# Multiplying by w_out with seven products of quarter sums, its weight sums made ahead

## The chip, the cores and the metric

The kernel runs on one core of a Trainium2 chip. The metric is the device time of one execution in microseconds (us). Three timed runs of the kernel before gave 1209.68, 1209.86 and 1210.95 us, so its median is 1209.86 us. A separate profiled execution gives the spans, waits and durations below. Engines are named as in the profile: PE (matrix products and transposes), PEld (its weight loads), DVE (vector arithmetic), ACT (copies and functions), POOL (a second, slower elementwise engine), SP (the queue that issues nearly every DMA). SBUF is the on-chip memory, PSUM the eight banks that PE writes into; a bank holds 128 x 512 numbers.

## What is computed

```python
h = concat(meta_tokens, x)                       # 16 + 1024 tokens, width 1024
# mixer, on u = rmsnorm(h)
z = u @ w_in                                     # split: a, q, k, v, r, lr, ga, gb
y_a = (pool(a) @ w_pool_mix * pool_scale) @ w_pool_out
o   = rmsnorm(gla_chunked(q, k, v, log_a)) * silu(r)
y_b = o @ w_gla_out
m   = sigmoid(ga) * y_a + sigmoid(gb) * y_b      # 1024 x 1024
h   = h + m @ w_out                              # the product that is changed
# MLP
h   = h + square(relu(rmsnorm(h) @ w_ff1)) @ w_ff2
out = rmsnorm(h)[16:]
```

All of it is float32. A product is taken as three passes: each operand is split into a high part (rounded) and a low part (the rest), and high x high, high x low and low x high are added in one bank (`mm3`, lines 281 to 287). So every 128 x 128 x 512 block costs three matmuls, and every operand costs one ACT copy for the high part and one subtraction for the low part.

## The kernel before

The program is written as a list of steps. PE runs in the order in which the steps are written; for the other engines the framework's scheduler chooses an order, with earlier code first. An instruction passed through `keep_in_program_order` is placed behind the instruction that was written before it on the same engine.

**Stage one** (steps `one`, until about 385 us). Norm, transposes, the value projection, then four `a_block`s, two `decays`, four `mix_block`s and two `k_block`s (line 720), and then `pairs_of_projections` (line 853), which already takes its part of `w_in` by seven products of sums (Strassen's scheme in Winograd's form). `differences` (line 692) makes the sums of the input that these products need; the tile pair `t2h`, `t2l` (for the product called P4) is one of them. Weights come through a ring of depth two (`Ring`, lines 57 to 94) by way of two buffers `raw`.

**Attention** (`gla`, line 1277). While PE waits inside the recurrence, it is given filler: four `ya_block`s and four `yb_block`s for the first half of the tokens (h=0). A `yb_block(j, h)` (line 1172) makes two 128-wide columns of m for 512 tokens: twelve matmuls each, then on DVE `gl = (1+gl)*b` (L1195) and `gl += ml` (L1196), then the split: ACT high part (L1199), DVE low part (L1200). `gl` and `ml` are pairs of 256 KB tiles that `ask` (line 1127) loads into a set of small buffers; it always leaves two of these free.

**The merge and w_out** (steps `rest`, from `merge_open`, line 1313, to about 588 us). Eight small buffers hold the pairs (`t1`, `o`). PE takes the four `yb_block`s of the second half of the tokens (h=1, order 2, 3, 0, 1) and sixteen `out_tile(t, ch)` (line 1362): 128 tokens by 512 columns, eight blocks deep, 24 matmuls each, 384 in all. `load_wo` splits w_out in eight pieces of 128 x 1024: ACT L1344, DVE L1345. Bank group `mm` has three banks, `ms` three. `out_tile` adds the bank to x in `acc` (L1379); after the second column half `layer_norm` and `turn_tile` (line 1386, eight transposes) prepare the quarter sums for w_ff1.

**MLP** (`ff1`, `ff2`). Both products go by seven products of sums. PE runs them without a gap but for the first fifteen microseconds.

Of the kernel before, what the change touches and what calls it, by code (L numbers as in the profile page):

```python
# [14 lines left out]
P = 128  # L15
# [81 lines left out]
class Raw:  # L97
# [11 lines left out]
    def load(self, ap, n):  # L109
# [13 lines left out]
def kernel(  # L123
# [55 lines left out]
    h_dram = dp.tile([8, P, D], F32, name="h_dram")  # L179
    hf_dram = [dp.tile([NPAIR, P, HALF], F32, name=f"hf{m}_dram") for m in range(7)]  # L180
# [425 lines left out]
    def decays(p):  # L606
        def fn():
# [6 lines left out]
            if p:  # L614
                act.activation(gnorm, gnorm, ACT.Copy, scale=0.5)
# [6 lines left out]
    def pool_open():  # L622
# [4 lines left out]
        lr_turn()  # L627
        act.activation(S["gu"], wgu, ACT.Copy)
# [91 lines left out]
    for f, i in ((a_, 0), (d_, 0), (a_, 1), (d_, 1), (m_, 0), (a_, 2), (m_, 1), (a_, 3), (m_, 2), (k_, 0), (m_, 3)):  # L720
        f(i)
# [365 lines left out]
    def gla_open():  # L1087
        left.pop_to(S["left_t"])
        right.pop_to(0)
        S["yg"] = {h: right.push(f"yg{h}", [P, 2, HEADS, HALF], F32R) for h in (1, 0)}  # L1090
# [9 lines left out]
        wanted[:] = [("a", d, h) for d in range(8) for h in range(2)] + [("b", d, 0) for d in range(8)]  # L1100
# [67 lines left out]

    KEPT = (2, 3)
    kept = {}  # L1170

    def yb_block(j, h):
        def fn(wb=None):
# [7 lines left out]
            yg = S["yg"][h]  # L1181
            for e in range(2):
                d, w = 2 * j + e, slice(e * P, (e + 1) * P)
                ask()
                gl, ml = take("b", d, h)
# [11 lines left out]
                th = MH[h][:, d]  # L1197
                tl = ML[h][:, d]
                act.activation(th, gl, ACT.Copy, scale=0.5)  # L1199
                dve.scalar_tensor_tensor(tl, gl, 0.5, f32(th), ALU.mult, ALU.subtract)  # L1200
# [132 lines left out]

    def load_wo(ch, kk):
        def fn():
            wo = S["wo"][ch][:, :, 2 * kk : 2 * kk + 2]
            c = slice(ch * HALF, (ch + 1) * HALF)
            src = w_out[kk * 256 : (kk + 1) * 256, c].rearrange("(k p) c -> p k c", p=P)
            if ch:
                r = raw.load(src, D).rearrange("p (k c) -> p k c", k=2)  # L1340
            else:
                r = S["acc"][:, 4 + kk].rearrange("p (k c) -> p k c", k=2)
                nc.sync.dma_start(r, src)
            act.activation(wo[:, 0], r, ACT.Copy)  # L1344
            dve.tensor_tensor(wo[:, 1], r, f32(wo[:, 0]), ALU.subtract)  # L1345
# [3 lines left out]
    step(rest, merge_open)
    def wo1_open():  # L1350
        raw.back()
        left.pop_to(S["left2"])
        right.pop_to(0)
        S["u2p"] = right.push("u2p", [P, 2, HALF], F32)
        raw.lend(right.push("rawx0", [P, D], F32))
        S["right_ff"] = right.mark()
        S["wo"].append(right.push("wo1", [P, 2, KT, HALF], F32R))


    ORDER = (0, 4, 1, 5, 2, 3, 6, 7)  # L1360

    def out_tile(t, ch):
        def fn():
            half, at = t // 4, (t % 4) * P
            wo = S["wo"][ch]
            if ch == 0 and t < 6:
                x_again(t + 2)
# [371 lines left out]
```

## Time and profile before

| | |
|---|---|
| median of the timed runs | 1209.86 us (1209.68 to 1210.95) |
| the profiled execution | span 1209.1 us from its first to its last instruction, 18303 instructions; no other time is given for it |
| busy | PE 1194.4, PEld 993.1, DVE 837.5, ACT 574.4, POOL 79.1 us |
| mean granted clock of PE | 0.998 |
| w_out matmuls (L285, L286, L287 with `wo`) | 128 each, from 490.1 to 587.9 us |
| yb matmuls, both halves (with `yg`) | 64 each for three lines, from 447.3 us |

A line of a group reads: line in the code, engine, operation, output <- inputs, shape, count | busy us, mean ns of one | idle time before it and who ended it. A line of the timeline reads: start us, duration us, engine, line, and so on, and in brackets the idle time before it with its releaser. Matmul ends are modelled, so what counts for PE is the distance from one start to the next.

### The profile page before, as it was taken

The page shows a single profiled execution, that of the slowest core. Times are in us where ns is not written, and L with a number is a line of the kernel's source. Part 1 is how long each engine was busy: PE and PEld are TensorE (multiplying, and loading weights), DVE is VectorE, ACT ScalarE, POOL GpSimd, SP SyncE. Part 2 cuts the span into 40 slices and gives each one's busy share as a digit, 9 for nine tenths or more (in the row PEclk, how much of TensorE's full clock was granted, in tenths as well). Part 3 has the DMA queues.
Part 4 walks back from the last instruction along what each step waited for, and adds up shares of the span by engine and source line. Part 5 has one row for each costly group of instructions (what it writes and reads, how often), then busy time and mean ns, then how long its engine had stood idle before and what let it go on. Part 6 is the DMA issues. An engine that isn't in the chain of part 4 may idle for free.

```text
span 1209.1 us, 18303 instructions
## 1 busy us (share of the span) xinstructions
PE 1194.4 (99%) x6775; PEld 993.1 (82%) x6775; DVE 837.5 (69%) x1369; ACT 574.4 (48%) x1014; POOL 79.1 (7%) x97
## 2 busy tenths in 40 slices
PE   9999999999999999999999999999999999999997
PEld 7999877878778887788788888888888888888886
DVE  6636567565686669726887767677675887887686
ACT  7546444444456124305655545455464444444554
POOL 0000062323320000000000000000000000000000
PEclk9999999999999999999999999999999999999999
DMA  8223253534348978812255444444479963333532
GB/s 245 77 60 123 91 133 110 166 110 146 112 138 296 315 218 268 284 32 87 88 161 168 151 139 157 148 160 151 152 253 318 348 229 98 98 100 91 173 96 88
DMA packets 151385, 192.79 MB, mean 159 GB/s; under 512 B 12216, under 2 KB 86256, under 8 KB 151296
## 3 DMA queue, kind: packets, MB, share of 16 engines
q1 hardware_dynamic: 151136, 191.56, 49.5%
q8 instruction: 53, 0.87, 0.3%
q14 instruction: 36, 0.29, 0.1%
q10 hardware_dynamic: 160, 0.07, 0.0%
HBM read 128.66 MB, written 62.93 MB: 158 GB/s over the span
## 4 chain that ended last, share of the span: by engine, by line
PE 68%; DVE 3%; issue 1%; DMA 1%; ACT 1%; DVEq 0%; ACTq 0%
PE b_oa L287 5%; PE b_oa L285 5%; PE b_oa L286 5%; PE b_y L285 4%; PE b_y L286 4%; PE b_y L287 4%; PE b_mm L285 4%; PE b_mm L287 4%; PE b_mm L286 4%; PE b_ob L287 4%; PE b_ob L285 4%; PE b_ob L286 4%; PE b_z L286 3%; PE b_z L285 3%; PE b_z L287 3%; PE b_sc L285 2%
## 5 line engine op out<-in xcount | busy, mean ns | idle before, releaser
L774 ACT ACTIVATE w1h<-raw 128x512 fp32r<-128x512 f32 x106 | 65.8, 622 | 51.2 <-PE b_sc L286 21.2
L285 PE MATMUL b_sc<-th,w1h 128*128 128x512 f32 x216 | 85.4, 395 | 0.4 <-ACT u2p L1522 0.4
L285 PE MATMUL b_z<-th,w1h 128*128 128x512 f32 x216 | 84.9, 393 | 0.4 <-DVE c L893 0.4
L775 DVE TENSOR_TENSOR w1l<-raw,w1h 128x512 fp32r<-128x512 f32 x106 | 72.5, 685 | 18.0 <-ACT w1h L774 18.0
L286 PE MATMUL b_sc<-tl,w1h 128*128 128x512 f32 x216 | 84.8, 393 | 0.0
L286 PE MATMUL b_z<-tl,w1h 128*128 128x512 f32 x216 | 84.2, 390 | 0.4 <-DVE tl L1408 0.4
L287 PE MATMUL b_sc<-th,w1l 128*128 128x512 f32 x216 | 84.4, 391 | 0.0
L287 PE MATMUL b_z<-th,w1l 128*128 128x512 f32 x216 | 84.1, 389 | 0.0
L774 ACT ACTIVATE w1h<-fs 128x512 fp32r<-128x512 f32 x81 | 51.1, 630 | 67.0 <-PE b_y L286 33.6
L775 DVE TENSOR_TENSOR w1l<-fs,w1h 128x512 fp32r<-128x512 f32 x81 | 57.7, 712 | 23.7 <-ACT w1h L774 23.7
L285 PE MATMUL b_mm<-th,w1h 128*128 128x512 f32 (+1 forms) x208 | 72.0, 346 | 0.0
L287 PE MATMUL b_mm<-th,w1l 128*128 128x512 f32 (+1 forms) x208 | 71.1, 342 | 0.0
L286 PE MATMUL b_mm<-tl,w1h 128*128 128x512 f32 (+1 forms) x208 | 71.0, 342 | 0.0
L774 ACT ACTIVATE w1h<-bt 128x512 fp32r<-128x512 f32 x46 | 29.1, 632 | 70.8 <-issue 43.9
L1598 DVE TENSOR_TENSOR bt<-w,w 128x512 f32<-128x512 f32 x80 | 54.7, 683 | 2.7 <-DMA w<-in_w_ff_dram 2.7
L285 PE MATMUL b_mm<-wo,th 128*128 128x512 f32 x128 | 50.4, 394 | 0.9 <-PE b_mm L287 0.9
L287 PE MATMUL b_mm<-wo,tl 128*128 128x512 f32 x128 | 49.9, 390 | 0.0
L286 PE MATMUL b_mm<-wo,th 128*128 128x512 f32 x128 | 49.8, 389 | 0.0
L285 PE MATMUL b_y<-wo,w1h 128*128 128x512 f32 x128 | 49.8, 389 | 0.0
L286 PE MATMUL b_y<-wo,w1h 128*128 128x512 f32 x128 | 49.8, 389 | 0.0
L287 PE MATMUL b_y<-wo,w1l 128*128 128x512 f32 x128 | 49.8, 389 | 0.0
L775 DVE TENSOR_TENSOR w1l<-bt,w1h 128x512 fp32r<-128x512 f32 x46 | 31.8, 691 | 25.6 <-ACT w1h L774 25.6
(425 smaller groups left out, 3317.1 us busy)
## 6 DMA issues: line engine op xcount, KB each, us to landing
hf_dram<-h SPq DMA_DIRECT2D x112, 256.0 KB, 2.1
raw<-hf_dram SPq DMA_DIRECT2D x112, 256.0 KB, 2.6
w<-in_w_ff_dram SPq DMA_DIRECT2D x64, 256.0 KB, 4.8
raw<-in_w_in_dram SPq DMA_DIRECT2D x22, 512.0 KB, 4.7
raw<-in_w_ff_dram SPq DMA_DIRECT2D x16, 512.0 KB, 4.1
rawx<-in_w_ff_dram SPq DMA_DIRECT2D x16, 512.0 KB, 4.1
rawp<-in_w_in_dram SPq DMA_DIRECT2D x10, 512.0 KB, 4.2
xs<-in_x_dram SPq DMA_DIRECT2D x8, 512.0 KB, 4.8
```

The costliest lines, as they stand in the source:

```text
L285: pe.matmul(ps, ah, bh, start=first and i == 0, stop=False, skip_group_check=more)
L286: pe.matmul(ps, ah, bl, start=False, stop=False, skip_group_check=more)
L287: pe.matmul(ps, al, bh, start=False, stop=last and i == n - 1, skip_group_check=more)
L774: act.activation(hi, a, ACT.Copy)
L775: dve.tensor_tensor(lo, a, f32(hi), ALU.subtract)
L1598: dve.tensor_tensor(bt, w, S["w2"][q[3:]][:, i], ALU.add if q[2] == "+" else ALU.subtract)
```

## The change

- w_out is taken by seven products P1 to P7 of 512 x 512 quarters, each four tiles of 128 tokens, four blocks deep, twelve matmuls per tile: 7 x 4 x 12 = 336 matmuls in place of 384. The second half of the tokens forms the first row of quarters, the first half the second row; `tokens()` maps rows back for x and the output.
- The weight sums T1 to T4 are made in stage one, on POOL, from sixteen 256 KB loads of w_out (`wo_load`, `wo_sums`, `wo_parts`, `wo_store`), and kept in DRAM (`ws_dram`): T1 and T2 already split, T3 and T4 whole. These steps stand between the blocks of stage one; the loads, the ACT copies and the stores are pinned.
- Each column of m is now split and also added or subtracted into the sums that the products need: for h=0 in `yb_block`, for h=1 in `after_half1`. One column quarter (A21) goes to DRAM and back.
- The blocks of w_gla_out take columns j and j+4 instead of 2j and 2j+1.
- The pairs `gl`, `ml` of the second half use four small buffers instead of eight. Bank groups become `mm` two, `x` two, `ms` two.
- P5, P2, P3, P7 and P4 are added to `acc` by DVE; P1 and P6 share a bank, are copied out by ACT and added by POOL.
- `turn_tile` gives one subtraction to POOL, and one of its two splits moves into `ff_room`.

```diff
+    def wo_sums(k):
+        b11, b12, b21, b22 = (S["wr"][:, k % 2, j] for j in range(4))
+        for to, a, b in ((b11, b12, b11), (b12, b22, b12), (b22, b22, b11), (b21, b21, b22)):
+            in_two(ALU.subtract, to, a, b)
...
+    o_((LOAD, 0), (LOAD, 1), (SUM, 0))
+    a_(0)
+    o_((SUM, 1))
+    d_(0)
+    o_((PART, 0))
+    a_(1)
+    d_(1)
+    o_((PART, 1))
+    m_(0)
+    o_((STORE, 0), (LOAD, 2), (SUM, 2))
+    a_(2)
+    o_((STORE, 1), (LOAD, 3))
+    m_(1)
+    o_((SUM, 3), (PART, 2))
+    a_(3)
+    m_(2)
+    o_((STORE, 2), (PART, 3))
+    k_(0)
+    o_((STORE, 3))
+    m_(3)
...
                 dve.scalar_tensor_tensor(gl, gl, 1.0, b, ALU.add, ALU.mult)
                 dve.tensor_tensor(gl, gl, ml, ALU.add)
-                act.activation(th, gl, ACT.Copy, scale=0.5)
-                dve.scalar_tensor_tensor(tl, gl, 0.5, f32(th), ALU.mult, ALU.subtract)
+                if h:
+                    after_half1(j, e, gl)
+                elif e == 0:
+                    nc.sync.dma_start(a21_dram[j], gl)
+                else:
+                    split_to(quarter(1), j, gl)
+                    dve.tensor_tensor(gl, gl, m[0], ALU.add)
+                    split_to(quarter(2), j, gl)
...
+    def after_half1(k, e, m):
+        s2, s3 = S["acc"][:, 4 + k, :HALF], S["tmp"][:, k]
+        if e == 0:
+            split_to(quarter(3), k, m)
+            in_two(ALU.subtract, s3, m, s3)
+            dve.tensor_tensor(s2, s2, m, ALU.subtract)
+            split_to(far(1), k, s2)
+            split_to(quarter(0), k, s3)
+        else:
+            split_to(S["w"][1], k, m)
+            in_two(ALU.subtract, s2, m, s2)
...
+        S["io"] = [S["u2"][:, i, c] for i in range(2) for c in halves()]
...
+    def staged(p, slots, eng=dve):
+        what, (hi, lo) = WEIGHTS[p], weights_of(p)
+        for k, a in enumerate(slots):
+            nc.sync.dma_start(a, wo_rows(...) if what[0] == "b" else ws_dram[...])
+        for k, a in enumerate(slots):
+            act.activation(hi[:, k], a, ACT.Copy)
+            if eng is pool:
+                in_two(ALU.subtract, lo[:, k], a, f32(hi[:, k]))
             else:
+                dve.tensor_tensor(lo[:, k], a, f32(hi[:, k]), ALU.subtract)
...
+    yb(2)
+    later(x_column, 1, 1)
+    yb(3)
+    later(x_column, 0, 1)
+    out_products("P5", 0, 1, 2, 3)
+    later(lambda: staged("P2", [S["acc"][:, t, :HALF] for t in range(4)], pool))
+    yb(0)
+    later(x_column, 0, 0)
+    yb(1)
+    later(lambda: staged("P1", raw_halves()))
+    later(ready, "P6")
+    out_products("P2", 0, 1, 2, 3)
+    later(lambda: staged("P3", raw_halves(), pool))
+    later(fourth_sums)
+    out_products("P1", 0, 1, 2, 3)
...
+    out_products("P6", 0, 1)
+    out_products("P3", 0)
+    out_products("P6", 2)
+    out_products("P3", 1)
+    out_products("P6", 3)
+    later(turn_tile, 0)
...
+    later(turn_tile, 5)
+    out_products("P4", 3)
```

`in_two` is one POOL operation in two halves of 128 x 256; `split_to` is one ACT copy and one DVE subtraction of 128 x 512. The operands are as follows.

| product | tokens | weights |
|---|---|---|
| P5 | sum of the two h=0 columns | T1, loaded split from DRAM (`ready`) |
| P2 | second column of h=1 | b21 of w_out, split when P5 is done (low part on POOL) |
| P1 | first column of h=1 | b11, split (low part on DVE) |
| P6 | S2 | T2, loaded split |
| P3 | S4, made by `fourth_sums` | b22, split (low part on POOL) |
| P7 | S3 | T3, split (DVE) |
| P4 | second column of h=0 | T4, split (DVE) |

More of the change, by code (lines that the diff above doesn't have):

```diff
@@ L1089, in gla_open @@
         right.pop_to(0)
[L1090 removed]
+        S["fo"] = right.push("fo", [P, 2, KT, HALF], F32R)
+        S["yg"] = {h: S["fo"][:, :, 4 * (1 - h) : 4 * (2 - h)] for h in range(2)}
         buffer("o", 3, HALF, right)
@@ L1349 @@
[L1349 to L1367, printed above, removed]
-            if ch == 0 and t == 6:
-                act.activation(gB, gB, ACT.Copy, scale=-0.5)
-            b, n = bank("mm"), ORDER.index(t)
-            for j in range(2):
-                if ch and j and n > 1:
-                    turn_tile(ORDER[n - 2])
-                mm3(
-                    b, KT // 2, lambda i: (MH[half][:, 4 * j + i, at : at + P], ML[half][:, 4 * j + i, at : at + P]),
-                    lambda i: (wo[:, 0, 4 * j + i], wo[:, 1, 4 * j + i]), first=j == 0, last=j == 1,
-                )
-            a = S["acc"][:, t, ch * HALF : (ch + 1) * HALF]
-            dve.tensor_tensor(a, b, a, ALU.add)
-            if ch:
-                layer_norm(S["acc"][:, t], S["u2"][:, n % 2])
-                nc.sync.dma_start(h_dram[t], S["acc"][:, t])
-        return fn
@@ new lines, in raw_halves, with ready, product @@
+    def raw_halves():
+        return [t[:, c] for t in raw.own for c in halves()]
+    def ready(p):
+        what = WEIGHTS[p]
+        for k in range(4):
+            for u, a in enumerate(weights_of(p)):
+                nc.sync.dma_start(f32(a[:, k]), ws_dram[int(what[1]) - 1, k, u])
+    in_x = {}
+    def product(p, t):
+        (ah, al), (wh, wl), c = tokens_of(p), weights_of(p), slice(t * P, (t + 1) * P)
+        first = p in ("P1", "P2", "P5", "P3")
+        if p == "P1":
+            b = in_x[t] = bank("sc" if t < 2 else "x")
+        else:
+            b = bank("mm") if first else in_x[t]
+        mm3(b, 4, lambda k: (ah[:, k, c], al[:, k, c]), lambda k: (wh[:, k], wl[:, k]), first=first, more=not first)
+        (c11, c12), (c21, c22) = ([S["acc"][:, 4 * r + t, h] for h in halves()] for r in range(2))
+        if p in ("P1", "P6"):
+            copy, to = S["tmp"][:, t], c11 if p == "P1" else c12
+            act.activation(copy, b, ACT.Copy)
+            in_two(ALU.add, to, to, copy)
+            return
+        for to in {"P5": (c12, c22), "P2": (c11,), "P3": (c12,), "P7": (c22,), "P4": (c21,)}[p]:
+            dve.tensor_tensor(to, b, to, ALU.add)
+        if p in ("P3", "P4"):
+            finish_half(t if p == "P3" else 4 + t)
@@ L1437, in load_ff, with far_split, later, out_products @@
+    def far_split(n, cols, a):
+        fh, fl = (x[:, :, cols] for x in quarter(n))
+        act.activation(fh, a, ACT.Copy)
+        dve.tensor_tensor(fl, a, f32(fh), ALU.subtract)
+    def yb(j):
+        step(rest, yb_block(j, 1), *(() if j in KEPT else (W1, [two_columns(j)])))
+    def later(fn, *args):
+        step(rest, lambda: fn(*args))
+    def out_products(p, *tiles):
+        for t in tiles:
+            later(product, p, t)
     def load_ff(i, u):
         load_block(w_ff1, i, u, 2 * i * P)
-    def first_blocks():
+    def early_blocks():
```

208 lines of the change are left out of this document (132 added, 76 removed).

## The prediction

> **What bounds the kernel now.** I read the page first, then the table by stretches, then PE's timeline where a stretch has fewer matmuls than its length allows.
>
> ```profile
> span 1209.1 us, 18303 instructions
> PE 1194.4 (99%) x6775; PEld 993.1 (82%) x6775; DVE 837.5 (69%) x1369; ACT 574.4 (48%) x1014; POOL 79.1 (7%) x97
> 700.00:950.00 250.00, 250.00 (x1104) 207.01 (x1104) 173.46 (x274) 125.44 (x210) 0.00 (x0) 1.00 0.58 197
> 440.00:471.00 31.00, 30.85 (x216) 25.30 (x213) 25.92 (x42) 11.47 (x17) 0.00 (x0) 1.00 0.69 211
> 471.00:490.00 19.00, 17.36 (x76) 13.72 (x74) 16.80 (x23) 8.86 (x11) 0.00 (x0) 1.00 0.91 315
> 520.00:588.00 68.00, 68.00 (x326) 56.76 (x325) 35.75 (x65) 26.05 (x56) 0.00 (x0) 1.00 0.14 55
> ```
>
> PE bounds the kernel: it is busy 99% at a granted clock of 1.00. The stretch 700 to 950 holds nothing but 128x512 matmuls, so one costs 250.00/1104 = 0.2264 us from start to start. The modelled 389 ns of one overlap and are not its price. One tile of twelve costs 2.72 us, a yb_block of 24 costs 5.43.
>
> By that price 471 to 490 should hold 84 matmuls and holds 76. This is the stretch where the change works, and there DVE and the DMA engines (share 0.91) are nearly full as well. From 520 on w_out runs dense with DVE half idle and the DMA at 0.14. So work moved between engines costs nothing after 520 and may cost everything before.
>
> **The matmuls.** 384 become 336. 48 x 0.2264 = 10.9 us, all on PE's path: **-10.9**. The transposes stay (eight tiles, six of them inside the product).
>
> **Two old stalls.**
>
> ```profile
> 479.51 0.39 PE L287 MATMUL b_mm<-yg,w1l 128*128 128x512 f32 x1
> 480.80 0.50 PE L285 MATMUL b_mm<-yg,w1h 128*128 128x512 f32 x1 [0.90 <-DVE o L1195]
> 488.87 0.39 PE L287 MATMUL b_mm<-yg,w1l 128*128 128x512 f32 x1
> 490.12 0.47 PE L285 MATMUL b_mm<-wo,th 128*128 128x512 f32 x1 [0.87 <-PE b_mm L287]
> ```
>
> PE lost 1.29 - 0.23 = 1.06 us waiting for a bank that DVE had not emptied, and 1.25 - 0.23 = 1.02 us at the first w_out tile. DVE was splitting w_out then:
>
> ```profile
> 468.06 0.68 DVE L1195 SCALAR_TENSOR_TENSOR c<-c,b_mm 128x512 f32<-128x512 f32 x1
> 468.66 0.68 DVE L1196 TENSOR_TENSOR t<-t 128x512 f32<-128x512 f32 x1
> 472.26 0.68 DVE L1195 SCALAR_TENSOR_TENSOR o<-o,b_mm 128x512 f32<-128x512 f32 x1
> 474.79 0.62 ACT L1199 ACTIVATE th<-o 128x512 fp32r<-128x512 f32 x1
> 474.92 1.23 DVE L1345 TENSOR_TENSOR wo<-acc,wo 128x1024 fp32r<-128x1024 f32 x1 [0.58 <-ACT wo L1344]
> 476.06 0.68 DVE L1200 SCALAR_TENSOR_TENSOR tl<-o,th 128x512 fp32r<-128x512 f32 x1
> 480.07 0.68 DVE L1195 SCALAR_TENSOR_TENSOR o<-o,b_mm 128x512 f32<-128x512 f32 x1
> ```
>
> These splits go; I count both stalls as gone, **-2.1**, and charge what takes their place separately. A DVE operation of 512 columns costs 0.60 us from start to start (468.06 to 468.66), 0.68 alone; an ACT copy 0.62.
>
> **What DVE gets instead.** For h=0 a block has 7 DVE operations instead of 6: 4 x 0.60 = +2.4. For h=1 it has 9 instead of 6 (and one later): +7.2 over four blocks, 5.4 each beside PE's 5.43. P5 adds two per tile, 4.8. Gone are four splits of w_out here (four more later), 4.6. So DVE is as full as PE from 451 to about 507, without a reserve. That gives no sum yet; what ends last is at the two places that follow.
>
> **Before P5.** Two things hold it. First T1: its tiles are pushed on the right stack where `o` lay, and the last h=0 pair leaves `o` at 476.06 + 0.68, less the L1345 of 1.1 ahead of it, plus 2.4, so at about 478.0. Then eight loads of 256 KB are issued on SP, with the h=1 pairs, A21 and x beside them.
>
> ```profile
> acc<-in_x_dram SPq DMA_DIRECT2D x6, 512.0 KB, 6.5
> o<-gb_dram SPq DMA_DIRECT2D x6, 256.0 KB, 4.0
> t<-gb_dram SPq DMA_DIRECT2D x5, 256.0 KB, 5.4
> ```
>
> A load lands in 4.0 us here; 2 MB at 315/0.91 = 346 GB/s take 6.1. The eighth is in at 485.4 (issue 0.43 each, then 4.0) to 487. Undelayed, P5 would begin at about 470.9 + 2 x 5.43 = 481.8 and read the fourth block 2.0 later, at 483.8: 1.6 to 3.2 late.
>
> Second, the four small buffers: they hold two pairs, so pair 3 is loaded only when pair 1 has left. That is L1195 and L1196 (1.4), for an even pair a POOL subtraction of two halves, two issues (0.6) and 4.0 to 5.4 to land.
>
> ```profile
> 224.75 2.40 POOL L810 TENSOR_TENSOR fs<-fs,raw 128x256 f32<-128x256 f32 x2 [3.73 <-DVE w1l L775]
> 232.54 1.44 POOL L810 TENSOR_TENSOR fs<-rawp 128x256 f32<-128x256 f32 x2 [5.39 <-DMA rawp<-in_w_in_dram]
> ```
>
> Two halves on POOL cost 1.44 to 2.40, so the round is 7.4 to 9.8 us where PE makes two pairs in 5.43. With two banks in `mm` PE may run ahead by two tiles: P5's first tile needs the bank of pair 3, free 0.7 after that pair's L1195, which is -0.1 to +2.3 late, plus the lag of DVE behind PE (the last h=0 L1195 starts at 472.26, some 1 us after its matmuls, and 2.4 us of DVE work come in ahead of it; I take 1 to 3). The two causes overlap; I take **+3.0**, bounds 0.5 (T1 in time, no lag) and 5.3.
>
> **Before P2.** P2 reads the column that the last yb_block makes. At the least that is L1195, L1196, an ACT copy and a DVE subtraction, 0.7 + 0.7 + 0.6 + 0.7 = 2.7 and some 0.3 of handing over, less the first block of three matmuls (0.7): 2.3 us that nothing covers; the old order had tiles of the other token half there. Above that stands the round again. Call P5's end E. P2's low parts (eight POOL halves, 5.8 to 9.6) can start only at E + 0.8, since they overwrite P5's tokens; behind them on POOL stand the subtractions of yb(0), 1.4 to 2.4 each, and only these free the buffers of the last pair: E + 9.4 to E + 15.2. Then load (4.6 to 6.0) and 2.7: E + 16.7 to E + 23.9, against E + 11.5 undelayed. That gives 5.2 to 12.4. But the scheduler may let the subtractions of yb(0) pass P2's low parts, whose later blocks are not read at once; then 2.3 to 5 remain. I take **+5.0**, bounds 2.3 and 11.
>
> [...]
>
> **After P2.** P1's weights are split on DVE during P2, P3's low parts (8 POOL halves) and P1's additions (8 halves) take 11.5 to 19.2 us on POOL and have P1 and two tiles of P6, 16.3 us. `turn_tile` stands 6.3 us behind the tile it needs at the tightest (turn 1, turn 5); from a tile's L1379 to the end of L259 is 4.2:
>
> ```profile
> 544.83 0.69 DVE L1379 TENSOR_TENSOR acc<-b_mm,acc 128x512 f32<-128x512 f32 x1 [4.75 <-PE b_mm L287]
> 547.75 1.28 DVE L259 SCALAR_TENSOR_TENSOR u<-acc,small,gB 128x1024 f32<-128x1024 f32 x1
> 602.64 0.50 PE L286 MATMUL b_z<-tl,w1h 128*128 128x512 f32 x1 [0.41 <-DVE tl L1408]
> ```
>
> The last row is a stall of 0.6 at the start of the MLP behind `turn_tile`'s DVE chain, which now is two operations shorter. I take **+0.5**, bounds -0.6 and 2.
>
> **Stage one.** Sixteen loads, 48 POOL halves, eight ACT copies and 24 stores come in between 73 and 145 us. PE does not wait for them, if SP and ACT do not stand still: ring loads are issued about 11 us ahead of their split.
>
> ```profile
> 73.21 1.91 ACT L704 ACTIVATE t2h<-xr 128x2048 fp32r<-128x2048 f32 x1 [1.79 <-PE b_mm L287]
> 75.16 2.29 DVE L705 TENSOR_TENSOR t2l<-xr,t2h 128x2048 fp32r<-128x2048 f32 x1 [1.78 <-ACT t2h L704]
> 100.00 0.38 SPq L118 DMA_DIRECT2D raw<-in_w_in_dram  x1
> 110.96 1.06 ACT L84 ACTIVATE w1h<-raw 128x1024 fp32r<-128x1024 f32 x1 [1.74 <-PE b_mm L286]
> 151.85 0.40 PE L285 MATMUL b_y<-t2h,w1h 128*128 128x512 f32 x1
> ```
>
> A load of k=2 waits for the stores of k=0 to leave the same buffer, and may hold SP some 5 us; the 11 us cover that. What is moved is `t2h`, `t2l`: they were made at 73 and read at 151.85. They come to lie where the weight sums lay, so they wait for the last store. The POOL work is 48 x 0.72 to 1.20 = 35 to 58 us from about 78, with the two changes of buffers some 10 more: the last store lands between 128 and 150, and after k_0 at the earliest (about 140). With 1.9 + 2.3 us for the split the pair is ready at 144 to 154. I take **+0.7**, bounds 0 and 4.
>
> **Sum.** -10.9 - 2.1 + 3.0 + 5.0 + 0.5 + 0.7 = -3.8 us. The profiled execution has a span of 1209.1, and would have 1205.3. The median of the timed runs lies 0.8 above that span; I carry the difference over: 1209.9 - 3.8 = **1206.1 us**.
>
> **The rivals.**
> *The full gain* (0.18). Loads land early and POOL lets yb(0) pass: the terms are 0.5, 2.3, 0 and 0, sum -10.2, 1199.7 us. For it: DVE's load fits PE's to the tenth. Against it: the DMA share of 0.91 already; from 467 to 503 the new order moves pairs 4, A21 1, T1 2, x 3, b21 and b11 2, w_gla_out 1 and a norm 0.5 MB, 13.5 MB, which at 346 GB/s take 39 us.
> *Slower, by the ring of two pairs* (0.24). The round of a buffer, not PE, sets the time of the h=1 blocks: at 9.8 us and a lag of 3 it costs 5.3 before P5, and at POOL's slow price 11 before P2. -13.0 + 16.3 + 1.2 = +4.5, 1214.4 us. It decides from where the two terms together pass 11.8. For it: 5.4 us to land and 2.40 on POOL are both seen. [...] Against it: the second POOL row ran at 1.44, and P5 gives 10.9 us in which pairs 5 and 6 come free.
> *No difference* (0.21). The losses of the forecast, and stage one at its bound of 4 because P4's operand is late: -0.5, 1209.4 us. For it: 35 to 58 us of POOL in a window of 70. Against it: ACT and DVE have room at 140 to 150.
> That the products would not be made as described I can't see: 336 matmuls stand in the code.
>
> **How the numbers follow.** The forecast, that about a third of the gain stays (faster, 1202 to 1207.4), has 0.37. With the full gain that makes faster by more than 0.2% (2.4 us, about what a measurement of this kernel can tell from no change) 0.55, same 0.21, slower 0.24. The range leaves out the best tenth and the upper half of the slower case: 1200.5 to 1213.5.
>
> **What would show it.** Right: 336 matmuls with w_out's operands; the two stalls at 480 and 490 gone; one gap of PE of about 3 us before or in P5 with T1's load or a bank as releaser, and one of about 5 us after P2's first three matmuls, released by the DVE low part of the last column; no gap over 1 us from P1 to the MLP. In the changed kernel's list of waits POOL should stand behind the late loads of pairs. Wrong: no gap before P2 above 2.5 us (then the full gain), gaps in every h=1 block (the ring), or a gap of PE at 152 us (stage one). The time would be most wrong if the DMA engines, not a buffer, set the pace from 470 to 505: then the share would stand at 1.0 throughout.

## The result, and the profile after

The changed kernel takes 1266.66 us (median of four runs, 1265.46 to 1268.30) beside 1209.77 us for the kernel before on the same chip: 56.9 us slower, ratio 1.0471 with a 95% interval of 1.0456 to 1.0486. The forecast was 1206.1 us and a range up to 1213.5. Its profiled execution has a span of 1264.2 us at a mean granted clock of 0.981 (before 0.998).

The head of the page of the changed kernel: span, then each engine's busy time, share and instructions.

```profile
span 1264.2 us, 18598 instructions
PE 1203.9 (95%) x6727; PEld 993.2 (79%) x6727; DVE 867.9 (69%) x1397; ACT 593.1 (47%) x1055; POOL 183.6 (15%) x209
```

6775 - 6727 = 48: the matmuls went as forecast. PE no longer fills the span, and POOL has 104.5 us more. The table by stretches says where. First the kernel before, then the changed one; the columns after the stretch are its length, the busy time of PE, PEld, DVE, ACT and POOL, PE's granted clock, the DMA share, GB/s.

```profile
125.00:150.00 25.00, 25.00 (x156) 22.59 (x155) 15.52 (x14) 13.43 (x19) 0.00 (x0) 1.00 0.34 107
475.00:550.00 75.00, 73.23 (x322) 60.06 (x321) 37.95 (x52) 18.27 (x26) 0.00 (x0) 1.00 0.51 173
600.00:660.00 60.00, 59.59 (x262) 48.72 (x261) 48.40 (x78) 32.65 (x56) 0.00 (x0) 1.00 0.47 150
939.00:960.00 21.00, 21.00 (x94) 17.41 (x93) 18.81 (x32) 8.93 (x16) 0.00 (x0) 1.00 1.01 358
```

```profile
125.00:150.00 25.00, 20.58 (x112) 17.96 (x111) 15.04 (x11) 10.43 (x17) 22.62 (x20) 0.86 0.59 191
475.00:550.00 75.00, 51.53 (x184) 38.25 (x183) 50.77 (x69) 21.47 (x34) 29.57 (x32) 0.85 0.69 230
600.00:660.00 60.00, 51.74 (x235) 41.48 (x234) 47.47 (x83) 30.54 (x64) 9.95 (x8) 0.94 0.28 93
939.00:960.00 21.00, 14.08 (x52) 10.85 (x51) 10.43 (x16) 8.12 (x14) 0.00 (x0) 0.84 0.83 287
```

Four stretches lose. In each PE is not only idle, its clock is lower as well. PE's timeline of the changed kernel shows the long gaps; a gap is the distance to the next start less 0.23 us.

```profile
137.60 0.39 PE L294 MATMUL b_mm<-th,w1l 128*128 128x512 f32 x1
142.35 0.80 PE L292 MATMUL b_mm<-ph,mw 128*128 128x512 f32 x1 [4.36 <-ACT ph L681]
...
497.94 0.39 PE L294 MATMUL b_mm<-fo,w1l 128*128 128x512 f32 x1
504.29 0.79 PE L292 MATMUL b_mm<-fo,w1h 128*128 128x512 f32 x1 [5.96 <-DVE u L1277]
504.88 0.63 PE L293 MATMUL b_mm<-fo,w1h 128*128 128x512 f32 x1
505.31 0.63 PE L294 MATMUL b_mm<-fo,w1l 128*128 128x512 f32 x1
...
541.55 0.47 PE L294 MATMUL b_mm<-th,wo 128*128 128x512 f32 x1
548.41 0.79 PE L292 MATMUL b_mm<-th,wo 128*128 128x512 f32 x1 [6.39 <-ACT wo L1249]
...
941.90 0.39 PE L294 MATMUL b_z<-th,w1l 128*128 128x512 f32 x1
949.21 0.80 PE L292 MATMUL b_oa<-w1h 128*128 128x512 f32 x1 [6.92 <-ACT w1h L838]
```

Gaps of 4.5 us in stage one, 6.1 in the blocks with h=1, 6.6 ahead of P2, 7.1 at the start of ff2. Between them lie smaller ones: 3.2 at 477, 3.0 at 509, 1.8 at 516, 1.9 at 535, and from the end of P2 into the MLP 0.9, 2.1, 1.1, 1.1, 2.0, 3.0 and 1.7. After each of the seven gaps of 3.0 us and more the matmuls stand 505.31 - 504.88 = 0.43 us apart instead of 0.23, for 4 to 12 of them, so such a gap costs 0.8 to 2.4 us more than its length, some 11 us for the seven.

The same starts in both traces split the loss. The first product of the pairs starts at 158.2 instead of 149.0 us; the first matmul on `yg` at 457.8 instead of 447.6 (so +10.2); ff2 at 949.2 instead of 896.6 (+52.6); the last matmul at 1256.2 instead of 1201.0 (+55.2).

### The profile page after: what moved, and what is told of

It is laid out like the page before. It is cut to its first block, busy times and chain, and to the rows that moved or that the text cites. A ratio compares the mean times of both kernels' runs of the same rounds, so it can differ in the third digit from the quotient of the medians.

```text
span 1264.2 us, 18598 instructions
## 1 busy us (share of the span) xinstructions
PE 1203.9 (95%) x6727; PEld 993.2 (79%) x6727; DVE 867.9 (69%) x1397; ACT 593.1 (47%) x1055; POOL 183.6 (15%) x209
## 4 chain that ended last, share of the span: by engine, by line
PE 80%; DVE 7%; ACT 4%; POOL 4%; DMA 3%; issue 2%; SPq 1%; POOLq 0%; DVEq 0%; ACTq 0%
PE b_y L292 6%; PE b_y L294 6%; PE b_y L293 6%; PE b_oa L292 5%; PE b_oa L293 5%; PE b_oa L294 4%; PE b_mm L292 4%; PE b_mm L293 4%; PE b_mm L294 4%; PE b_sc L292 4%; PE b_sc L293 4%; PE b_sc L294 4%; PE b_z L292 4%; PE b_z L293 4%; PE b_z L294 4%; PE b_ob L293 3%
## 5 line engine op out<-in xcount | busy, mean ns | idle before, releaser
L838 ACT ACTIVATE w1h<-raw 128x512 fp32r<-128x512 f32 x114 | 70.8, 623 | 75.0 <-PE b_sc L293 35.9
L839 DVE TENSOR_TENSOR w1l<-raw,w1h 128x512 fp32r<-128x512 f32 x114 | 78.0, 686 | 26.3 <-ACT w1h L838 26.3
L292 PE MATMUL b_sc<-fo,w1h 128*128 128x512 f32 x128 | 51.0, 399 | 3.0 <-ACT u2p L1681 3.0
L294 PE MATMUL b_y<-th,w1l 128*128 128x512 f32 x128 | 49.9, 390 | 1.5 <-DVE w1l L839 1.5
L294 PE MATMUL b_sc<-fo,w1l 128*128 128x512 f32 x128 | 50.8, 397 | 0.0
L293 PE MATMUL b_sc<-fo,w1h 128*128 128x512 f32 x128 | 50.8, 397 | 0.0
L292 PE MATMUL b_y<-th,w1h 128*128 128x512 f32 x128 | 49.8, 389 | 0.0
L293 PE MATMUL b_y<-tl,w1h 128*128 128x512 f32 x128 | 49.8, 389 | 0.0
L292 PEld LDWEIGHTS b_z<-th,w1h 128*128 128x128 f32 x216 | 40.7, 188 | 9.8 <-DVE c L957 0.9
L292 PE MATMUL b_oa<-w1h 128*128 128x512 f32 x104 | 41.6, 400 | 6.9 <-ACT w1h L838 6.9
L1658 ACT ACTIVATE h<-h 128x512 f32<-128x512 f32 x48 | 30.3, 632 | 37.6 <-DVE h L1698 25.6
```

The source lines that it names most:

```text
L292: pe.matmul(ps, ah, bh, start=first and i == 0, stop=False, skip_group_check=more)
L293: pe.matmul(ps, ah, bl, start=False, stop=False, skip_group_check=more)
L294: pe.matmul(ps, al, bh, start=False, stop=last and i == n - 1, skip_group_check=more)
L838: act.activation(hi, a, ACT.Copy)
L839: dve.tensor_tensor(lo, a, f32(hi), ALU.subtract)
L1658: act.activation(h, h if b is None else b, ACT.Relu)
```

## The experiments

The theory after the trace was one cause for each place: in stage one ACT stands at a pinned copy for a POOL sum, in the merge four small buffers are too few, at the start of ff2 a load waits for memory that an operand still holds. The rivals were POOL and DVE in each other's way, POOL's and DVE's queues, and SP or the DMA engines. The times below are each kernel's median over that of the kernel before on the same chip (the changed kernel: +56.9); the intervals are of the ratio.

### Stage one: the pins, the sums, the order

ACT in the changed kernel, stage one:

```profile
128.90 0.69 ACT L687 ACTIVATE c<-b_sc,small 128x512 f32<-128x512 f32 x1
136.88 0.63 ACT L723 ACTIVATE ws<-wr 128x512 fp32r<-128x512 f32 x1 [7.30 <-POOL wr L708]
140.59 0.63 ACT L723 ACTIVATE ws<-wr 128x512 fp32r<-128x512 f32 x1 [3.07 <-POOL wr L708]
141.12 0.65 ACT L696 ACTIVATE c<-b_mm 128x264 f32<-128x264 f32 x2
141.66 1.15 ACT L681 ACTIVATE ph<-s 128x512 fp32r<-128x512 f32 x2
```

ACT waits 7.3 and 3.1 us for POOL; the evacuation of a bank (L696) and the split that PE waits for (L681) stand behind.

**s1_nopin.**

```diff
-            tc.keep_in_program_order(act.activation(hi, a, ACT.Copy))
+            act.activation(hi, a, ACT.Copy)
```

> One edit in stage one: the eight ACT copies of wo_parts are no longer pinned, the loads and stores still are. Theory A, ACT stands at a copy until POOL has made that sum, wherever the copy is placed: unpinned, the scheduler takes the copies a little earlier, so ACT waits as long or longer, the gap of PE near 137 us stays between 3 and 6 us and the time stays at 1264 to 1269 us. Theory B, the pins themselves hold ACT: the gap of 4.5 us and the cold clock behind it go, 1257 to 1259 us.

1263.00 us, +53.6 (ratio 1.0442, 1.0425 to 1.0459). Neither. ACT waited 17.9 us for POOL's sums in all, against 15.3 in the changed kernel, but mostly at places where PE had work. The gap of 4.5 us went; one of 2.1 us came at 98, behind another split on ACT (L681), and the pairs still start at 156.0, 7.0 late. Only 3.3 us came back.

**s1_none.**

```diff
     def wo_sums(k):
         b11, b12, b21, b22 = ...
-        for to, a, b in (...):
-            in_two(ALU.subtract, to, a, b)
+        return
```

> Leaves out the 32 POOL halves that make the weight sums (T1 to T4 then hold plain quarters of w_out); loads, ACT copies, POOL's low parts and stores stay. Theory A, the loss of stage one is ACT waiting for POOL's sums: the gap near 137 us goes, the granted clock of 125 to 150 us is back above 0.97, the pairs' first product starts at 149 to 151 instead of 158.2 us, and the time is 1257 to 1260 us. [...]

1257.39 us, +48.0 (1.0398, 1.0382 to 1.0413). The pairs start at 149.5 us. So making the sums costs nearly all of stage one's loss; the 40 loads and stores that stay, with sixteen halves for low parts on POOL, cost at most 0.5 us.

**s1_early.**

```diff
     a_(1)
+    o_((STORE, 0), (LOAD, 2))
     d_(1)
     o_((PART, 1))
     m_(0)
-    o_((STORE, 0), (LOAD, 2), (SUM, 2))
+    o_((STORE, 1), (LOAD, 3), (SUM, 2))
     a_(2)
-    o_((STORE, 1), (LOAD, 3))
     m_(1)
-    o_((SUM, 3), (PART, 2))
+    o_((SUM, 3))
     a_(3)
+    o_((PART, 2))
```

> Only the order of the steps of stage one changes: the stores of k=0 and 1 and the loads of k=2 and 3 stand one or two blocks earlier, the sums are written one block ahead of the ACT copies that read them; amounts, pins and engines stay. Theory A (ACT stands at a copy for a POOL sum that was started too late): no ACT copy of wo_parts waits more than 1 us for POOL, the gap near 137 us goes, and the time is 1257 to 1260 us. Rival (the amount of POOL work beside DVE, not its place): a gap of 2 us or more stays and the time is above 1262 us.

1262.63 us, +53.2 (1.0440, 1.0425 to 1.0456). The 7.3 us wait is gone, yet the pairs start at 155.6, 6.6 late: the rival holds. Its trace has the reason, DVE, POOL and PE in order of time:

```profile
108.03 4.23 POOL L708 TENSOR_TENSOR wr<-wr 128x256 f32<-128x256 f32 x6 [9.35 <-DMA wr<-in_w_out_dram]
108.16 0.64 DVE L1021 TENSOR_TENSOR metab<-metab 128x8 f32<-128x8 f32 x1
108.83 0.66 DVE L1022 TENSOR_TENSOR metab<-metab 128x8 f32<-128x8 f32 x1
...
112.10 0.48 PE L292 MATMUL b_mm<-ph,mw 128*128 128x512 f32 x1
114.92 0.50 PE L293 MATMUL b_mm<-ph,mw 128*128 128x512 f32 x1 [2.33 <-DVE ph L682]
```

An operation of eight columns takes DVE 0.17 us elsewhere and 0.66 here, and each starts 0.67 to 0.70 us after the one before; POOL's halves take 4.23/6 = 0.70. Eight such in a row put off the low part that PE waits for. That gives theory E: each half on POOL holds up the DVE instruction that stands beside it until the half has ended, so a row of small ones on DVE moves at POOL's pace.

**s1_dve** puts E to the test, **s1_beside** takes it alone.

```diff
+    def in_one(op, to, a, b):
+        dve.tensor_tensor(to, a, b, op)
...
-            in_two(ALU.subtract, to, a, b)
+            in_one(ALU.subtract, to, a, b)
...
-            in_two(ALU.subtract, a.bitcast(F32R), a, f32(hi))
+            in_one(ALU.subtract, a.bitcast(F32R), a, f32(hi))
```

> Only in stage one: the weight sums and low parts of wo_sums and wo_parts are made by DVE (24 operations of 512 columns, some 0.6 us each, 14.4 us) instead of 48 halves on POOL; order and pins as in the changed kernel. Theory E, each POOL half holds DVE's two-input instructions until it ends (tiny 128x8 operations took 0.66 us instead of 0.17 beside it), and this is what the early order could not mend: the pairs' first product starts at 150 to 152.5 us instead of 158.2 and the time is 1258 to 1261 us. Theory A alone (ACT waits for sums that come late): some gain as with the early order, 1261.5 to 1264 us. Rival D, DVE has no room for 14.4 us more: 1265 us or above.

1255.89 us, +45.9 (1.0378, 1.0363 to 1.0394), better than expected; the pairs start at 149.7. The same sums on DVE cost 0.7 us at most, though DVE works for PE and POOL does not. (The 11.0 us that came back are more than the 9.2 that stage one had lost by the start of the pairs; the intervals are some 1.8 us to either side.)

The second edit is made in the kernel of the first:

```diff
     def in_one(op, to, a, b):
         dve.tensor_tensor(to, a, b, op)
+        in_two(op, *(S["idle"][:, i] for i in (2, 0, 1)))
```

> The kernel whose weight sums DVE makes in stage one (1255.9 us), and beside it 48 POOL halves of 128x256 on a scratch tile that nobody reads or waits for; they run from about 71 us, one behind the other. Theory E (POOL's halves hold DVE's instructions, whoever needs their result): DVE's tiny 128x8 operations take 0.6 to 0.7 us instead of 0.17 and its 128x1024 ones up to 1.7 instead of 1.22 while the halves run, and PE loses 1 to 5 us from 72 to 115 us: 1257 to 1261 us. Theory A alone (only waiting for POOL's results costs): within 1 us of 1255.9.

1265.87 us, +56.1 (1.0471, 1.0453 to 1.0488): 10.2 us for POOL work that nobody reads, twice what E had expected. The pairs start at 160.8. POOL, DVE and PE of this kernel:

```profile
99.59 4.66 POOL L710 TENSOR_TENSOR idle<-idle 128x256 f32<-128x256 f32 x6
100.83 0.67 DVE L1027 TENSOR_TENSOR metab<-metab 128x8 f32<-128x8 f32 x1
...
109.12 1.65 DVE L677 TENSOR_TENSOR s<-s 128x1024 f32<-128x1024 f32 x1
111.92 0.39 PE L294 MATMUL b_mm<-th,w1l 128*128 128x512 f32 x1
119.65 0.79 PE L292 MATMUL b_mm<-ph,mw 128*128 128x512 f32 x1 [7.34 <-ACT ph L683]
123.33 0.17 DVE L1026 TENSOR_TENSOR metab<-metab 128x8 f32<-128x8 f32 x1
124.05 1.22 DVE L85 TENSOR_TENSOR w1l<-raw,w1h 128x1024 fp32r<-128x1024 f32 x1
```

POOL's last half ended at 123.3; from that moment the eight columns cost 0.17 again and 1024 columns 1.22 instead of 1.65. The gap of 7.5 us at 112 names ACT as releaser, and ACT had waited 9.6 us for DVE.

### The merge: buffers or POOL

**m8.**

```diff
-        S["io"] = [S["u2"][:, i, c] for i in range(2) for c in halves()]
+        S["io"] = [S["u2"][:, i, c] ...] + [S["acc"][:, t, :HALF] for t in range(4)]
...
-    later(lambda: staged("P2", [S["acc"][:, t, :HALF] for t in range(4)], pool))
+    later(lambda: staged("P2", raw_halves(), pool))
...
-    later(x_column, 0, 0)
     yb(1)
-    later(lambda: staged("P1", raw_halves()))
+    later(lambda: staged("P1", [S["u2"][:, i, c] ...]))
+    later(x_column, 0, 0)
```

> Eight small buffers for the pairs instead of four (the first column half of four tiles of acc is lent to them; the raw b21 then goes through raw, the raw b11 through u2, x of c11 comes in later). Theory A, the ring of two pairs sets the pace of the blocks with h=1: the gaps of PE at 498 (6.1), 509 (3.0), 516 (1.8) and 535 us (1.9) shrink to less than half of their sum of 12.8 us, and with the cold clock behind them the time falls by 10 to 20 us, to 1247 to 1257 us. Rival, POOL's queue (eight additions of merge_open ahead of the first subtraction) or DVE sets the pace: the gaps stay and the time falls by less than 5 us.

1264.43 us, +55.0 (1.0458, 1.0429 to 1.0487): more buffers alone do not mend it. The gap at 498 kept its 6.1 us. The one of 3.0 at 509 went, but one of 3.1 came at 517: with eight buffers more pairs are asked for ahead, so SP stands 3.5 us for a pair's buffer with the loads of x for P5's sums queued behind it, and the first of those landed only at 518.5.

```profile
518.56 2.48 DVE L1494 TENSOR_TENSOR acc<-b_mm,acc 128x512 f32<-128x512 f32 x4 [2.50 <-DMA acc<-in_x_dram]
```

So m8 does not price the ring of four buffers by itself. DVE and POOL of the changed kernel show why the 6.1 us stayed:

```profile
492.88 7.41 POOL L708 TENSOR_TENSOR acc<-th,tl 128x256 f32<-128x256 f32 x8 [113.47 <-PE b_mm L294]
496.43 1.23 DVE L1250 TENSOR_TENSOR tl<-u,th 128x512 fp32r<-128x512 f32 x1
500.25 1.40 POOL L708 TENSOR_TENSOR tmp<-u,tmp 128x256 f32<-128x256 f32 x2
502.35 0.69 DVE L1250 TENSOR_TENSOR tl<-tmp,th 128x512 fp32r<-128x512 f32 x1 [4.69 <-ACT th L1249]
503.56 0.68 DVE L1277 SCALAR_TENSOR_TENSOR u<-u,b_mm 128x512 f32<-128x512 f32 x1
```

POOL takes the eight halves of merge_open's additions first, then the subtraction that DVE's queue already stands at (through ACT's copy of `tmp`); L1277, which frees PE's bank, is third in that queue. Ten us later DVE stands again, this time for ACT. SP, DVE and PE of the changed kernel, one after the other:

```profile
501.68 0.32 SPq L1202 DMA_DIRECT2D u<-gb_dram  x1
510.48 1.23 DVE L85 TENSOR_TENSOR w1l<-raw,w1h 128x1024 fp32r<-128x1024 f32 x1 [3.05 <-ACT w1h L84]
511.62 0.68 DVE L1277 SCALAR_TENSOR_TENSOR u<-u,b_mm 128x512 f32<-128x512 f32 x1
512.40 0.47 PE L292 MATMUL b_mm<-wo,th 128*128 128x512 f32 x1 [2.62 <-issue]
```

The pair that this L1277 adds was issued at 501.7 and 502.0 and had landed at 505.3. What L1277 stands behind is the split of the next weights (L85). Its high part is an ACT copy (L84), made at 509.4, when PE had done with the weights before. So the 3.0 us ahead of P5 are the order of DVE's queue, not a late pair; the waits of 1.8 at 516 and 1.9 at 535 come in the same way, from splits that wait for POOL's subtraction. In the changed kernel a pair was late only from 540 on, ahead of P2.

**m_dve** and **m8_dve.**

```diff
-            in_two(ALU.add, S["acc"][:, 4 + k, :HALF], f32(h), f32(l))
+            dve.tensor_tensor(S["acc"][:, 4 + k, :HALF], f32(h), f32(l), ALU.add)
...
-            in_two(ALU.subtract, s3, m, s3)
+            dve.tensor_tensor(s3, m, s3, ALU.subtract)
```

> POOL is taken out of the merge: merge_open's eight halves of additions become four DVE operations, and the two subtractions of each block with h=1 become one DVE operation each (twelve DVE operations, some 7.2 us, more on DVE); four small buffers as in the changed kernel. Theory C, DVE works its queue in order and stands at the split of tmp until POOL has subtracted, and POOL's first subtraction stands behind the eight additions: the gap of PE at 498 us (6.1) falls below 1.5 us, the one before P2 (6.6) below 4, and the time falls by 10 to 18 us, to 1249 to 1257 us. Theory A, the ring of two pairs sets the pace by itself: gaps of together more than 8 us stay from 495 to 545 us, now released by DVE with a late load behind it, and the time falls by less than 6 us. Rival D, DVE is full: the 7.2 us more on DVE show as gaps and the time does not fall.

> The edits of eight small buffers and of POOL taken out of the merge, together. If the ring of two pairs is the next limit once POOL is gone, this is at least 4 us faster than with POOL taken out alone; if DVE's queue was the whole cause, the two are within 2 us of one another (1249 to 1257 us).

m_dve 1259.53 us, +50.0 (1.0415, 1.0398 to 1.0433); m8_dve 1257.71, +48.2 (1.0397, 1.0382 to 1.0413). Seven us, less than theory C had expected: the gap at 498 fell to 1.0, but another wait came up behind it, for a pair (SP, PE, DVE and PE again):

```profile
502.53 0.32 SPq L1202 DMA_DIRECT2D u<-gb_dram  x1
503.50 0.39 PE L294 MATMUL b_mm<-fo,w1l 128*128 128x512 f32 x1
506.66 0.68 DVE L1277 SCALAR_TENSOR_TENSOR u<-u,b_mm 128x512 f32<-128x512 f32 x1
507.44 0.47 PE L292 MATMUL b_mm<-wo,th 128*128 128x512 f32 x1 [3.55 <-issue]
```

P5's first matmul needs the bank that L1277 frees. The pair for it was issued at 502.5, behind T1's eight loads and 1.9 us for its buffer, and landed at 506.5. T1's first pieces, all that this matmul reads of T1, had landed at 500.6 and 501.6. So here the ring of two pairs does hold PE: 3.7 us before P5. The gap ahead of P2 stayed at 6.1. Eight buffers take 1.8 us off m_dve, within what was set for no difference, and the two intervals overlap. In m8_dve the 3.7 fell to 1.2, but x came late here too (a gap of 4.0 at 511). What the ring costs is therefore left open.

**all_dve** gives DVE also the low parts of P2's and P3's weights, the additions of P1 and P6 and turn_tile's subtraction (in `in_two`, one `dve.tensor_tensor`; `staged(..., pool)` without `pool`).

> All POOL work that the change brought in goes to DVE: stage one, merge_open, the pairs, the low parts of the weights of P2 and P3, the additions of P1 and P6, turn_tile. Theory E (POOL holds DVE): -7 for the merge as measured with POOL out of the merge, -6 to -8 for stage one and -3 to -5 from P2 to the MLP, together 1246 to 1251 us; the gaps of PE at 574 (2.1) and 641 us (3.0) shrink below 1.2. Rival D (DVE becomes the bound): the gaps from 545 to 660 us grow, and the time is 1254 us or above.

1244.02 us, +34.0 (1.0283, 1.0268 to 1.0299): 22.9 us for leaving POOL out, more than expected though DVE has all of its work. Of the two gaps named, the one at P6 fell only from 2.1 to 1.4. The one of 3.0 at the MLP's first product went, but the wait of 1.7 for weights some 80 matmuls later grew to 3.1.

**m_skip** leaves work out.

```diff
                     split_to(quarter(1), j, gl)
-                    dve.tensor_tensor(gl, gl, m[0], ALU.add)
-                    split_to(quarter(2), j, gl)
...
-            in_two(ALU.subtract, s3, m, s3)
-            dve.tensor_tensor(s2, s2, m, ALU.subtract)
-            split_to(far(1), k, s2)
-            split_to(quarter(0), k, s3)
```

> Leaves out the sums of m: S1 of the first half (addition and split), S2 and S3 of the second half (subtractions and splits); merge_open's additions go to DVE, everything else stays, the four small buffers too. Theory D, DVE's and POOL's elementwise work for these sums and the standing in order behind it make the gaps of the merge: the gaps of PE from 470 to 545 us fall from some 27 us together to below 10, and the time to 1243 to 1252 us. Theory A, the ring of four small buffers: with shorter rounds but the same loads gaps of more than 12 us stay, 1255 us or above.

1249.65 us, +39.7 (1.0335, 1.0318 to 1.0352), inside theory D's bounds and 10.3 below m_dve (merge_open's additions are on DVE here too). But the gaps from 470 to 545 still make 13.3 us together, 2.9 of them before P5 and 3.0 + 4.0 before P2. More than 12 is what theory A had said of the gaps, so this run speaks for D by its time alone.

### The start of ff2

**f_swap.**

```diff
-        (t1h, t1l), (b22h, b22l) = (... quarter(q)] for q in (0, 1))
+        (t1h, t1l), (b22h, b22l) = (... quarter(q)] for q in (0, 2))
...
-        far_split(2, cols, lo)
+        far_split(1, cols, lo)
...
-        S["x"] = {..., "P3": quarter(1), "P6": quarter(2), ...}
+        S["x"] = {..., "P3": quarter(2), "P6": quarter(1), ...}
```

> One edit: in the MLP the operands of P3 and P6 change places in memory, so that the first 32 KB that w_ff2 is loaded into hold operands whose last reader is the last P6, three products of 2.72 us ahead of the end of ff1, and not the last P3, which is the last product. Theory A, the gap of 7.1 us at the start of ff2 is the load of w_ff2 waiting for that memory: the loads start about 8 us earlier against the end of ff1, the gap shrinks below 1 us, and the time falls by 7 to 9 us, to 1257.5 to 1259.5 us. Rival, the load waits for SP or for the DMA engines (stores of the hidden values, their reloading): the gap stays above 4 us and the time falls by less than 4 us.

1258.33 us, +48.9 (1.0408, 1.0393 to 1.0424): as expected. The first load of w_ff2 and the first product of ff2, in this kernel (SP's queue, then PE):

```profile
936.15 0.33 SPq L1738 DMA_DIRECT2D w<-in_w_ff_dram  x1
943.99 0.39 PE L294 MATMUL b_z<-th,w1l 128*128 128x512 f32 x1
944.21 0.39 PE L292 MATMUL b_oa<-w1h 128*128 128x512 f32 x1
```

In the changed kernel that load is issued at 942.10, when the last P3 has started its last matmul, since w_ff2's first 32 KB lie where P3's operands lay; here it is issued 8.1 us ahead of ff2, and no gap is left. In the kernel before the operands of P1 and P2 lay there, and it was issued at 885.16, 11.4 us ahead.

### Together

**combo_a**: s1_early, m_dve, f_swap, turn_tile's subtraction on DVE, and

```diff
-    out_products("P2", 0, 1, 2, 3)
-    later(lambda: staged("P3", raw_halves(), pool))
-    later(fourth_sums)
     out_products("P1", 0, 1, 2, 3)
+    out_products("P2", 0, 1, 2, 3)
+    later(lambda: staged("P3", raw_halves(), pool))
+    later(fourth_sums)
```

> Together: the early order of stage one, POOL out of the merge, the changed places of the MLP's operands, turn_tile's subtraction back on DVE, and the four tiles of P1 ahead of those of P2 (so that P1 covers the chain of the last column that P2 reads). If each loss is a place of its own and they add up: -8 (stage one), -12 (merge), -8.3 (start of ff2, as measured), -2 (turn_tile), -4 (before P2) = 1232 us, 1224 to 1240 us. If they share one cause (DVE full from 460 to 660 us), less: above 1245 us.

1246.30 us, +36.8 (1.0299, 1.0280 to 1.0319): the time that was set for one common cause, but not by it. The parts alone had given 3.7 (s1_early), 6.9 (m_dve) and 8.0 (f_swap), together 18.6; here it is 20.1. They add up within the noise, though the combination has P1's new place and turn_tile's subtraction besides, which no run has alone; 8 for stage one and 12 for the merge were set too high. The gap ahead of the products fell from 6.1 us to 2.0: P1 does cover the last column's chain. New waits of 3.3 at 582 (turn_tile) and 3.1 in the MLP came up.

**combo_b**: all_dve, s1_early, f_swap, P1 first, and T1 loaded ahead of the tmp tiles into the other of the two `wo` tiles.

```diff
+        ready("P5")
         for k in MERGE:
             nc.sync.dma_start(S["tmp"][:, k], a21_dram[k])
-        ready("P5")
```

> Together: nothing of the change on POOL, the early order of stage one, the changed places of the MLP's operands, P1's tiles ahead of P2's, and T1 loaded ahead of the tmp tiles into the buffer that does not lie where o lay. If the losses add up: 1246.3 as measured for the first combination, -4 for stage one, -3 for T1, -3 for P3 and P6 without POOL = 1236 us, 1231 to 1241 us. If DVE is full from 460 to 660 us: 1246 us or above.

1224.93 us, +15.0 (1.0122, 1.0107 to 1.0137). The losses add up, by more than was set: the time is below the range that was given for that. The wait before P5 stayed at 3.7 us, for a bank that waits for a late pair, as in m_dve. T1 loaded earlier changed nothing that can be seen there, since T1 was not what P5 waited for.

**combo_c, combo_d, combo_e, combo_f** changed the order in that kernel. In c, e and f the sum S1 is added from buffers that have been loaded again by then, so S1 is another and its addition waits for those loads.

```diff
-                    dve.tensor_tensor(gl, gl, m[0], ALU.add)
-                    split_to(quarter(2), j, gl)
+                    owed_sums.append((j, gl, m[0]))
...
-    out_products("P5", 0, 1, 2, 3)
+    out_products("P5", 0, 1)
     yb(0)
+    out_products("P5", 2, 3)
```

> The second combination (1224.9 us), and in the blocks with h=0 the addition and split that make S1 are written half a block later, behind the next block's first column, so that the split of the next weights stands ahead of them on ACT and DVE. Theory D (order on ACT and DVE, no amount): the gap of PE at 467 us (3.2, with 0.7, 0.7 and the cold clock some 8 us behind it) falls to below 1 us, and the time to 1217 to 1220 us. Rival (DVE is simply full from 460 to 483 us): the stall only moves to the next block, and the time stays at 1223 to 1226 us.

> The second combination, and P5's four tiles stand in two pairs between the last three blocks with h=1 instead of together. Theory A (a ring of two pairs: the blocks of PE come faster than buffers come free unless other work stands between them): the stalls at 492 us (3.7, a bank that waits for a late pair), 500 (1.2) and 522 us (1.5) fall to below 3 us together, 1220 to 1222 us. Rival (T1's load or P1's weights are what is late): they stay or move to P1, 1224 us or above.

> Both edits, the later S1 and the spread P5, together. If the two losses are separate the gains add: 1213 to 1217 us; if both draw on the same full DVE, no better than the better of the two alone.

> As the one before it, and eight small buffers for the pairs. If the ring of four still costs time once POOL is gone and the sums stand later, 2 to 4 us below the one before it; if not, within 1.5 us of it (with POOL taken out of the merge only, eight buffers gave 1.8 us).

combo_c 1223.18 us, +13.2 (1.0108, 1.0090 to 1.0126); combo_d 1228.09, +18.1 (1.0146, 1.0130 to 1.0163); combo_e 1231.10, +21.1 (1.0172, 1.0147 to 1.0197); combo_f 1227.86, +17.9 (1.0141, 1.0117 to 1.0165). Order does not mend it. combo_f, which has eight buffers, is 3.2 us below combo_e, as was expected if the ring still costs time; but the two intervals overlap. In c the stall at 467 us stayed (3.5), which speaks for a full DVE, but not cleanly, because of those loads. In d the wait before P5 stayed (3.9) and P1's weights became late (3.0).

**combo_g** is combo_b with m_skip's lines left out.

> The second combination (1224.9 us) without the sums of m: leaves out S1 of the first half (addition and split) and S2 and S3 of the second half (subtractions and splits). Theory D (what is left is DVE's and ACT's work for these sums, in a stretch where DVE has no idle): the stalls from 460 to 525 us (some 19 us with the cold clock) fall to below 8, 1211 to 1216 us. Rival (loads, the ring of four, the gate before the products): 1219 us or above.

1214.73 us, +5.0 (1.0043, 1.0028 to 1.0058): 10 us for the sums of m, in theory D's bounds by the time, and the same 10 as from m_dve to m_skip. Like m_skip it leaves the sums out, so it is no version of the product. The stretch of the last blocks with h=0 in the kernel before, combo_b and combo_g, one line each:

```profile
455.00:475.00 20.00, 19.85 (x96) 16.23 (x95) 18.62 (x27) 8.74 (x12) 0.00 (x0) 1.00 0.76 242
```

```profile
455.00:475.00 20.00, 16.12 (x68) 12.10 (x67) 17.83 (x24) 7.58 (x10) 0.00 (x0) 0.88 0.95 303
```

```profile
455.00:475.00 20.00, 19.22 (x92) 15.78 (x91) 16.66 (x22) 5.51 (x7) 0.00 (x0) 1.00 0.92 300
```

DVE has 18.6 of 20 us already before the change, with 96 matmuls. With the new sums PE gets 68 matmuls done in the same time, without them 92, and DVE's time per matmul is 0.19, 0.26 and 0.18 us. The DMA share is as high in both, which speaks against the DMA engines' rate; but it does not show DVE's work as the one cause. In combo_b the stall at 467 ends with ACT's copy of the next weights:

```profile
468.55 0.63 ACT L1249 ACTIVATE th<-o 128x512 fp32r<-128x512 f32 x1 [2.58 <-DVE o L1286]
469.08 1.04 ACT L84 ACTIVATE w1h<-raw 128x1024 fp32r<-128x1024 f32 x1
470.18 0.79 PE L292 MATMUL b_mm<-fo,w1h 128*128 128x512 f32 x1 [3.05 <-ACT w1h L84]
```

PE was ready at 467.0 and the weights landed at 467.2; from then to 468.5 ACT stood at the high part of the new sum, waiting for DVE, with the weights' copy behind it. So here the new sum holds PE through ACT's queue, and without the sums ACT has fewer copies too. That they cost 10 us is measured; how the 10 us divide is not.

## Why the prediction was wrong, point by point

- **The matmuls**, 48 fewer at the same 0.2264 us from start to start: right, and the only term in it that shortens the kernel by much.
- **Two old stalls**: they went, but the last block with h=0 still waits 0.94 us for a bank.
- **Before P5, +3.0**: the gap at P5's first matmul is 3.0 us, and that is luck, for neither of the two causes in the sum made it. The pair and T1's first pieces were in; DVE stood at the split of the next weights. What was not in the sum at all are the 6.1 us ahead of it, merge_open's additions: on DVE (m_dve) 1.0 is left. The step that failed is "a POOL subtraction of two halves", taken at its own duration without asking what stands ahead of it in POOL's queue and behind it in DVE's. The late pair, the second cause named, showed only once POOL was out of the way (3.7 in m_dve, all_dve, combo_a and combo_b).
- **Before P2, +5.0**: 6.6. Right in kind, the round of a buffer: the last pair landed at 545.0, 4.8 us after its block's last matmul, and the column's chain came behind it (3.4 us to PE's next start). Nearly right in size too, though the working's own 5.2 to 12.4 would have given a higher term. Without POOL (all_dve) 5.0 remain: the pair landed 4.0 us after that matmul, and PE went on 2.4 later. With eight buffers as well (m8_dve) the pair came early, and 4.9 remain, with splits of weights ahead of the column.
- **After P2, +0.5**: wrong. The seven gaps make 11.8 us; 8.6 without POOL, some 6.9 in combo_b. They end with ACT's copies and DVE's operations, and were not told apart.
- **Stage one, +0.7 with a bound of 4**: wrong, 9.2. The step that failed is "PE does not wait for them, if SP and ACT do not stand still": ACT does stand, 7.3 and 3.1 us at copies pinned behind POOL's sums, and even without the wait of 7.3 (s1_early) DVE's operations on eight columns take 0.66 us instead of 0.17 beside POOL's halves. t2h, which the text worried over, was in time.
- **DVE as full as PE, "that gives no sum yet"**: it did. The blocks with h=0 lost 3.2 + 0.7 + 0.7 + 0.9 us and some 2 of slow clock, and combo_g puts the sums of m at 10 us in the mended kernel.
- **The start of ff2** was not looked at: 8.0 us (f_swap). What the operands of the last products held in memory was changed by the new places of the quarters, and no view of the old trace shows that but the time of the load.
- **The clock**: the sum counted gaps at their length. The seven of 3.0 to 7.1 us cost 0.8 to 2.4 more each, some 11 together.

The rival "slower, by the ring of two pairs" had the sign, but its +4.5 us are far from +56.9. Its late pair is there, before P2 and, once POOL is out, before P5; its price was not measured cleanly (1.8 and 1.9 us in the m8 runs and 3.2 in combo_f, all with overlapping intervals). The prediction priced POOL's halves at their own length, 1.44 to 2.40 us for two, while what they cost lay on DVE (0.66 us instead of 0.17 for eight columns). Over the runs: leaving POOL out gives 22.9 us (11.0 in stage one, 6.9 in the pairs and merge_open, the remaining 5 from P2 on), ff2's start 8.0, the sums of m 10. The rest of combo_b's gain, about 11 us by subtraction, goes with the new orders and with what they shift; no visible part of it is T1's load. What is left in combo_g is 5.0 us above the kernel before, where 10.9 fewer was to be had: nine stalls of 0.6 to 2.4 us, 12.8 together, which were not told apart. No version came out below the kernel before.

## What to carry to other kernels

Elementwise work given to POOL is not free because POOL is idle: look at what DVE does at that moment, since in these runs it paid for POOL's instructions (48 halves that nobody reads cost 10.2 us in s1_beside). When an engine gets a new instruction to wait for, read what is queued behind it, and what is queued ahead on the engine that it waits for. And when operands change places, look at what is loaded into that memory next, hundreds of microseconds later.

## What the runs showed of the hardware

- While POOL ran 128x256 operations back to back (s1_beside), a DVE operation on eight columns took 0.66 us instead of 0.17 and one on 1024 columns 1.65 instead of 1.22. The excess of the small one, 0.49 us, stays under the length of a POOL half, 0.70 in s1_early. By what means POOL slows DVE was not shown.
- After the seven gaps of 3.0 to 7.1 us of the changed kernel the matmuls stood 0.43 us apart instead of 0.23, for up to 6.4 us, and the granted clock was 0.84 to 0.94 in the stretches that hold them. The length of a gap alone does not tell whether this follows: in combo_g it followed gaps of 2.4 us at 476 and 1.9 at 514, but not one of 2.1 at 539, and in the changed kernel it did not follow those of 1.8 to 2.1.
